# An 8192x8192 fp32 transpose: 16 KB store reads, and loads written as sixteen 512-byte runs into a column-major, 256-byte-aligned input buffer

## Chip, cores, metric

One core of one Trainium2 chip (trn2). The metric is device time in microseconds (us) of the whole kernel, as a median of several executions. Lower is better.

## The reference

```python
def setup_inputs():
    return {"x": np.random.randn(8192, 8192).astype(np.float32)}

def reference(x):
    return np.transpose(x)
```

256 MiB have to be read and 256 MiB written: 537 MB in all through the core's 16 DMA engines.

## The kernel before

The matrix is worked off in 32 blocks of 1024 rows x 2048 columns (8 MB). A block is loaded in two DMAs of 4 MB on the SP queue. The input buffer lies in SBUF, the core's memory of 128 partitions. In each partition a matrix row of 2048 floats is 8 KB, read in one piece and written in one piece. (A contiguous piece that a DMA writes is called a write run below.) The tensor engine (PE) transposes 128x128 squares against an identity into PSUM, the buffer that it writes; ScalarE (ACT) and VectorE (DVE) take turns to copy PSUM into `out_tile`; every four column groups ACT issues a 2 MB store. There are two input buffers and four output buffers.

```python
    R = 8;  C = 16;  I = R * P;  J = C * P;  G = 4;  LS = 2
    in_pool  = ctx.enter_context(tc.tile_pool(name="in_pool", bufs=2))
    out_pool = ctx.enter_context(tc.tile_pool(name="out_pool", bufs=4))
    # [...] const pool, PSUM pool of 4, identity
    for bj in range(n_bj):
        for bi in range(n_bi):
            in_tile = in_pool.tile([P, R, J], dt)                  # row-major
            rs = R // LS
            for s in range(LS):                                    # two loads of 4 MB
                src = x[i0 + s * rs * P:i0 + (s + 1) * rs * P, j0:j0 + J]
                src = src.rearrange("(a p) j -> p a j", p=P)
                nc.sync.dma_start(out=in_tile[:, s * rs:(s + 1) * rs, :], in_=src)
            for g in range(C // G):
                out_tile = out_pool.tile([P, G, I], dt)
                for bb in range(G):
                    # [...] 8 transposes of in_tile[:, a, b*P:(b+1)*P] into ps
                    # [...] ACT or DVE copies ps to out_tile[:, bb, :]
                dst = out[j0 + g * G * P:j0 + (g + 1) * G * P, i0:i0 + I]
                dst = dst.rearrange("(b q) i -> q b i", q=P)
                nc.scalar.dma_start(out=dst, in_=out_tile)         # 2 MB, 4 KB pieces
```

As built, a store's access patterns are `[[4096,128],[1024,4],[1,1024]]` on the SBUF side and `[[8192,128],[1048576,4],[1,1024]]` on the DRAM side: both sides in pieces of 1024 floats, 4 KB, although the SBUF side is one contiguous run of 16 KB in each partition. All SBUF tiles start 128 bytes past a multiple of 256.

## Time and profile before

| | before |
|---|---|
| time | 1278.35 us (1277.52 to 1279.18, 2 runs) |
| profiled span | 1276.3 us |
| bytes moved | 537.5 MB, mean 421 GB/s |
| DMA packets | 32768 of 8 KB (loads), 65536 of 4 KB (stores) |
| busy: PE / DVE / ACT | 55% / 25% / 20% |

The page of the kernel before. The DMA and GB/s lines have one entry for each fortieth of the span: the busy share of the 16 DMA engines in tenths, and what they moved. Under "DMA queue", q1 carries the loads and q10 the stores; the last column is the time that their packets took, as a share of 16 engines' span. Part 4 is the chain of work that ended last.

```profile
span 1276.3 us, 9511 instructions
...
DMA  9999999999999999999999999999999999999999
GB/s 392 425 423 424 425 423 425 423 422 424 423 422 423 424 424 423 424 422 423 424 424 422 422 422 424 424 423 423 423 423 424 422 422 422 424 424 423 422 422 375
...
q10 hardware_dynamic: 67584, 268.44, 51.4%
q1 hardware_dynamic: 33792, 268.44, 49.8%
...
DMA 89%; PE 6%; DVE 3%; issue 0%; ACT 0%; DVEq 0%; ACTq 0%; SPq 0%
...
```

The engines are busy in every slice, and the two queues' packets add up to 101.2% of the span, a little over 100% because neighbouring packets overlap. Apart from the first and last slice nothing is left but the rate itself, 422 to 425 GB/s.

Two stretches of the kernel before in the windows view (bounds in us, length, busy time and number of instructions of PE, of PE's weight loads, of DVE, ACT and POOL, then granted PE clock, DMA share, GB/s): a steady one and the last 37 us.

```profile
...
40.00:640.00 600.00, 332.62 (x1912) 298.34 (x1912) 145.36 (x120) 115.76 (x119) 0.00 (x0) 0.72 1.02 423
1240.00:1277.00 37.00, 15.20 (x126) 13.30 (x123) 9.80 (x8) 8.10 (x8) 0.00 (x0) 0.81 0.91 374
...
```

The longest waits of the kernel before (engine, line, what it waited for: us in total, times, longest):

```profile
...
ACT out_tile L69 <- DMA out_dram<-out_tile: 832.2, 97, 14.2
...
DVE out_tile L71 <- DMA out_dram<-out_tile: 593.7, 81, 11.7
...
PE ps L63 <- DMA in_tile<-in_x_dram: 25.0, 3, 13.0
...
```

The copies wait for stores to free an output buffer. PE almost never waits for input (25.0 us in 3 waits). So input is ahead of need and output is what lags.

Besides these views the trace records every DMA packet with its queue, start, size and duration. There is one data packet for each piece read, however it is written. They are remarkably uniform, and I use them throughout as "packet records": here 8 KB load packets have a median of 309 ns and 4 KB store packets one of 159 ns.

### The profile page before, as it was taken

How to read it: one execution, taken by the hardware profiler on the slowest of the kernel's cores; microseconds unless marked ns; L12 is line 12 of the kernel's file. 1: busy time of each engine (PE TensorE's matmuls, PEld its weight loads, DVE VectorE, ACT ScalarE, POOL GpSimd, SP SyncE). 2: the span in 40 equal slices, each digit the busy share in tenths (PEclk: the TensorE clock that was granted, in tenths of full speed). 3: DMA queues.
4: the chain of work that ended last, by engine and by line, in shares of the span. 5: the costliest groups of instructions: out<-in, count | busy, mean ns of one | idle time of the engine just before them, and what ended most of it. 6: DMA issues, size and time to landing. Idle time of an engine off the chain costs nothing.

```text
span 1276.3 us, 9511 instructions
## 1 busy us (share of the span) xinstructions
PE 700.7 (55%) x4096; PEld 629.0 (49%) x4096; DVE 313.5 (25%) x256; ACT 252.8 (20%) x257; POOL 0.7 (0%) x6
## 2 busy tenths in 40 slices
PE   3555555655565545655556555555555655556463
PEld 3454455544554544544445554454444544445453
DVE  1222223222232222322123221222222322122222
ACT  1221112121121211212112121221211212112121
POOL 0000000000000000000000000000000000000000
PEclk8777777767777677776677766878667777677867
DMA  9999999999999999999999999999999999999999
GB/s 392 425 423 424 425 423 425 423 422 424 423 422 423 424 424 423 424 422 423 424 424 422 422 422 424 424 423 423 423 423 424 422 422 422 424 424 423 422 422 375
DMA packets 101418, 537.49 MB, mean 421 GB/s; under 512 B 3072, under 2 KB 3072, under 8 KB 68608
## 3 DMA queue, kind: packets, MB, share of 16 engines
q10 hardware_dynamic: 67584, 268.44, 51.4%
q1 hardware_dynamic: 33792, 268.44, 49.8%
q8 instruction: 32, 0.52, 0.1%
q14 instruction: 10, 0.08, 0.0%
HBM read 268.44 MB, written 268.44 MB: 421 GB/s over the span
## 4 chain that ended last, share of the span: by engine, by line
DMA 89%; PE 6%; DVE 3%; issue 0%; ACT 0%; DVEq 0%; ACTq 0%; SPq 0%
DMA out_dram<-out_tile 87%; PE ps L63 6%; DVE out_tile L71 3%; DMA in_tile<-in_x_dram 2%; ACT out_tile L69 0%; DVEq L71 0%; ACTq L69 0%; SPq L55 0%
## 5 line engine op out<-in xcount | busy, mean ns | idle before, releaser
L63 PE MATMUL ps<-ident,in_tile 128*128 128x128 f32 x4096 | 700.7, 344 | 560.5 <-DVE out_tile L71 535.3
L63 PEld LDWEIGHTS ps<-ident,in_tile 128*128 128x128 f32 x4096 | 629.0, 181 | 631.9 <-DVE out_tile L71 605.9
L71 DVE COPY out_tile<-ps 128x1024 f32<-128x1024 f32 x256 | 313.5, 1225 | 948.9 <-DMA out_dram<-out_tile 593.7
L69 ACT COPY out_tile<-ps 128x1024 f32<-128x1024 f32 x256 | 251.5, 1014 | 1007.1 <-DMA out_dram<-out_tile 832.2
L69 ACT ACT_TABLE_LOAD x1 | 1.3, 1283 | 0.7 <-PEq L91 0.7
masks.py:199 POOL TENSOR_SCALAR_AFFINE_SELECT ident<-ident 128x128 f32<-128x128 f32 x1 | 0.3, 292 | 0.1
masks.py:197 POOL MEMSET ident<- 128x128 f32 x1 | 0.2, 204 | 0.3 <-POOLq L91 0.3
L91 POOL MEMSET const-bfloat16-1.0<- 128x1 bf16 x1 | 0.1, 101 | 0.0
L91 POOL MEMSET const-uint8-127<- 128x1 uint8 x1 | 0.1, 101 | 0.0
L91 POOL MEMSET const-float32-0.0<- 128x1 f32 x1 | 0.1, 98 | 0.2 <-issue 0.2
L91 POOL MEMSET const-float32-1.0<- 128x1 f32 x1 | 0.1, 98 | 0.0
## 6 DMA issues: line engine op xcount, KB each, us to landing
in_tile<-in_x_dram SPq DMA_DIRECT2D x64, 4096.0 KB, 27.9
out_dram<-out_tile ACTq DMA_DIRECT2D x128, 2048.0 KB, 28.9
```

Of the source, the lines that this page charges most:

```text
L63: nc.tensor.transpose(ps[:, a * P:(a + 1) * P], in_tile[:, a, b * P:(b + 1) * P], ident,)
L69: nc.scalar.copy(out=out_tile[:, bb, :], in_=ps)
L71: nc.vector.tensor_copy(out=out_tile[:, bb, :], in_=ps)
L91: nc = _bacc.Bacc("TRN2", target_bir_lowering=False, num_devices=1)
```

## The change

The intent: fewer, larger reads. A hand-made access pattern keeps the long contiguous side of a DMA as one run instead of cutting it to the pieces of the other side. Stores then read 16 KB at once and write four 4 KB rows. Loads still read 8 KB rows, but the input buffer is now column-major (`[P, C, R, P]`), so a row is written as sixteen 512-byte runs that are 4 KB apart. A pad of 128 bytes moves all tiles to multiples of 256 bytes. A block is loaded by eight DMAs of 1 MB instead of two of 4 MB. Waits are written by hand, with the same numbers of buffers. PE, ACT and DVE work is the same.

```diff
+def wide_dma(nc, eng, queue, out, in_):      # a DMA whose two sides keep their own run lengths
+    return eng.add_instruction(mybir.InstDMACopy(mode="Copy", [...],
+        ins=[physical(in_)], outs=[physical(out)], queue=queue))
-    LS = 2
+    LS = R
+        nc.alloc_sbuf_tensor("pad", [P, 32], dt)
-            in_tile = in_pool.tile([P, R, J], dt)
+        ins = [nc.alloc_sbuf_tensor(f"in_tile{k}", [P, C, R, P], dt).ap() for k in range(NIN)]
-                nc.sync.dma_start(out=in_tile[:, s * rs:(s + 1) * rs, :], in_=src)
+                src = x[i0 + s * P:i0 + (s + 1) * P, j0:j0 + J]
+                ld = wide_dma(nc, nc.sync, "qSPDynamicHW", in_tile[:, :, s, :], src)
-                            in_tile[:, a, b * P:(b + 1) * P],
+                            in_tile[:, b, a, :],
-                nc.scalar.dma_start(out=dst, in_=out_tile)
+                    st = wide_dma(nc, nc.scalar, "qActDynamicHW", dst, outs[ob])
 # [...] semaphores by hand instead of tile pools; the first block's loads and the last store
 # [...] use dma_start (the loads come out with the same access patterns)
```

More of the change, by code (lines that the diff above doesn't have):

```diff
@@ L8, with physical @@
 from concourse._compat import with_exitstack
+def physical(ap):
+    t = ap.tensor
+    dims = [list(d) for d in ap.ap]
+    if len(dims) == 2:
+        dims.insert(1, [dims[1][1], 1])
+    return mybir.PhysicalAccessPattern(
+        ap=dims,
+        offset=ap.offset,
+        dtype=ap.dtype,
+        memref=t.name,
+        memsetref=t.name + "_set",
+    )
+def wide_dma(nc, eng, queue, out, in_):
+    return eng.add_instruction(
+        mybir.InstDMACopy(
+            mode="Copy",
+            name=nc.get_next_instruction_name(),
+            engine=eng.engine,
+            ins=[physical(in_)],
+            outs=[physical(out)],
+            queue=queue,
+        )
+    )
 @with_exitstack
@@ L29 @@
     G = 4
-    LS = 2
-    const_pool = ctx.enter_context(tc.tile_pool(name="const", bufs=1))
-    in_pool = ctx.enter_context(tc.tile_pool(name="in_pool", bufs=2))
-    out_pool = ctx.enter_context(tc.tile_pool(name="out_pool", bufs=4))
-    psum_pool = ctx.enter_context(tc.tile_pool(name="psum", bufs=4, space=bass.MemoryType.PSUM))
-    ident = const_pool.tile([P, P], dt)
-    make_identity(nc, ident)
-    n_bi = N // I
-    n_bj = M // J
-    copy_idx = 0
-    for bj in range(n_bj):
-        j0 = bj * J
-        for bi in range(n_bi):
-            i0 = bi * I
-            in_tile = in_pool.tile([P, R, J], dt)
-            rs = R // LS
-            for s in range(LS):
-                src = x[i0 + s * rs * P:i0 + (s + 1) * rs * P, j0:j0 + J]
-                src = src.rearrange("(a p) j -> p a j", p=P)
-                nc.sync.dma_start(out=in_tile[:, s * rs:(s + 1) * rs, :], in_=src)
+    LS = R
@@ new lines @@
+    NIN = 2
+    NOUT = 4
+    NPS = 4
+    with tc.tile_critical():
+        nc.alloc_sbuf_tensor("pad", [P, 32], dt)
+        ident = nc.alloc_sbuf_tensor("ident", [P, P], dt).ap()
+        ins = [nc.alloc_sbuf_tensor(f"in_tile{k}", [P, C, R, P], dt).ap() for k in range(NIN)]
+        outs = [nc.alloc_sbuf_tensor(f"out_tile{k}", [P, G * I], dt).ap() for k in range(NOUT)]
+        pss = [nc.alloc_psum_tensor(f"ps{k}", [P, I], dt).ap() for k in range(NPS)]
+        s_id = nc.alloc_semaphore("s_id")
+        s_ld = [[nc.alloc_semaphore(f"s_ld{k}_{s}") for s in range(LS)] for k in range(NIN)]
+        s_st = [nc.alloc_semaphore(f"s_st{k}") for k in range(NOUT)]
+        s_pe = nc.alloc_semaphore("s_pe")
+        s_cp = [nc.alloc_semaphore("s_cpa"), nc.alloc_semaphore("s_cpv")]
+        nc.gpsimd.memset(ident, 0.0).then_inc(s_id, 1)
+        nc.gpsimd.wait_ge(s_id, 1)
+        nc.gpsimd.affine_select(
+            out=ident,
+            in_=ident,
+            compare_op=mybir.AluOpType.not_equal,
+            fill=1.0,
+            base=0,
+            pattern=[[-1, P]],
+            channel_multiplier=1,
+        ).then_inc(s_id, 1)
+        nc.tensor.wait_ge(s_id, 2)
+        blocks = [(bi, bj) for bj in range(M // J) for bi in range(N // I)]
+        rs = R // LS
+        n = 0
+        ng = 0
+        NG = len(blocks) * (C // G)
+        for k, (bi, bj) in enumerate(blocks):
+            slot, use = k % NIN, k // NIN
+            i0, j0 = bi * I, bj * J
+            in_tile = ins[slot]
+            if k >= NIN:
+                nc.sync.wait_ge(s_pe, (k - NIN + 1) * C)
+            for s in range(LS):
+                src = x[i0 + s * P:i0 + (s + 1) * P, j0:j0 + J]
+                if k > 0:
+                    ld = wide_dma(nc, nc.sync, "qSPDynamicHW", in_tile[:, :, s, :], src)
+                else:
+                    ld = nc.sync.dma_start(
+                        out=in_tile[:, :, s, :], in_=src.rearrange("p (b c) -> p b c", c=P)
+                    )
+                ld.then_inc(s_ld[slot][s], 16)
@@ L57 @@
             for g in range(C // G):
-                out_tile = out_pool.tile([P, G, I], dt)
+                ob, ouse = ng % NOUT, ng // NOUT
+                ng += 1
                 for bb in range(G):
                     b = g * G + bb
-                    ps = psum_pool.tile([P, R * P], dt)
+                    ps = pss[n % NPS]
+                    e = n % 2
+                    eng = (nc.scalar, nc.vector)[e]
+                    if n >= NPS:
+                        nc.tensor.wait_ge(s_cp[(n - NPS) % 2], (n - NPS) // 2 + 1)
@@ L62 @@
                     for a in range(R):
-                        nc.tensor.transpose(
+                        if b == 0 and a % rs == 0:
+                            nc.tensor.wait_ge(s_ld[slot][a // rs], 16 * (use + 1))
+                        ins_t = nc.tensor.transpose(
                             ps[:, a * P:(a + 1) * P],
-                            in_tile[:, a, b * P:(b + 1) * P],
+                            in_tile[:, b, a, :],
                             ident,
                         )
-                    if copy_idx % 2 == 0:
-                        nc.scalar.copy(out=out_tile[:, bb, :], in_=ps)
-                    else:
-                        nc.vector.tensor_copy(out=out_tile[:, bb, :], in_=ps)
@@ L72 @@
-                    copy_idx += 1
+                    ins_t.then_inc(s_pe, 1)
+                    eng.wait_ge(s_pe, n + 1)
+                    if bb < 2 and ouse > 0:
+                        eng.wait_ge(s_st[ob], 16 * ouse)
+                    o = outs[ob][:, bb * I:(bb + 1) * I]
+                    if e == 0:
+                        c = nc.scalar.copy(out=o, in_=ps)
+                    else:
+                        c = nc.vector.tensor_copy(out=o, in_=ps)
+                    c.then_inc(s_cp[e], 1)
@@ L74 @@
+                    n += 1
                 dst = out[j0 + g * G * P:j0 + (g + 1) * G * P, i0:i0 + I]
+                nc.scalar.wait_ge(s_cp[0], n // 2)
+                nc.scalar.wait_ge(s_cp[1], n // 2)
                 dst = dst.rearrange("(b q) i -> q b i", q=P)
-                nc.scalar.dma_start(out=dst, in_=out_tile)
+                if ng < NG:
+                    st = wide_dma(nc, nc.scalar, "qActDynamicHW", dst, outs[ob])
+                else:
+                    st = nc.scalar.dma_start(out=dst, in_=outs[ob])
@@ L80 @@
+                st.then_inc(s_st[ob], 16)
+        for ob in range(NOUT):
+            nc.sync.wait_ge(s_st[ob], 16 * (ng // NOUT))
 _INS = ['x']
```

## The prediction

> **What bounds it now.** The DMA engines. The page's slices show DMA at 9 (90% or more) in all 40, and 422 to 425 GB/s in all but the first (392) and last (375); 537.5 MB move in the 1276.3 us span. The chain of waits is 89% DMA, almost all stores. PE is busy 55%, DVE 25%, ACT 20%; their waits (ACT 832 us, DVE 594 us for stores to free out_tile) are consequences.
>
> The packet records behind the queue table are very regular: an 8 KB load packet takes 309 ns, a 4 KB store packet 159 ns, a 4-byte semaphore packet 9 ns. So 4 KB take 150 ns, and each packet of either direction has a fixed cost of about 9 ns. In the steady stretch busy time sums to 101.7%, so neighbours overlap by 3.6 ns and about 5.9 ns count. The Trainium skill, "DMA: Bandwidth & Descriptors", section "Where 436 GB/s comes from", puts the ceiling at 435.2 GB/s; the packets' slope agrees. Estimate: 537 MB at that rate 1233.6 us, plus 6144 data packets per engine x 5.9 ns = 36 us, plus 6 to 8 us of ramp and tail = 1276 to 1278. This closes.
>
> **What the change does.**
> 1. Stores read 16 KB at once instead of four times 4 KB: 1024 instead of 4096 read packets per engine. DRAM runs stay 4 KB. If the fixed cost belongs to the read packet: -3072 x 5.9 ns = -18 us, all on the critical path.
> 2. Loads keep 8 KB reads (2048 packets per engine) but write sixteen 512-byte runs each: 32768 write runs per engine instead of 2048. If a packet is cut on the read side and its writes stream, cost near 0. Each nanosecond per run that does not hide costs 33 us. I think most of it hides.
> 3. SBUF tiles start 256-aligned instead of 128 bytes off. The same page, section "How a descriptor splits into AXI transactions", says an unaligned start costs extra beats. The trace has no aligned data packets, only a few instruction packets of 8 KB at 307 instead of 309 ns. Estimate: 0 to 4 ns of the 5.9 for the 3072 remaining packets, 0 to -12 us, say -5.
> 4. 256 loads of 1 MB instead of 64 of 4 MB: 192 more semaphore packets per engine, at most +2 us. Issuing stays hidden on the SP queue.
> 5. PE, DVE and ACT work is unchanged (4096 transposes, 256 copies), buffering too (2 inputs, 4 outputs). If the queues alternate by packet, 16 KB store packets now beat 8 KB load packets, the reverse of before. Input arrives later, and waits move from "copies wait for stores" to "PE waits for loads"; the engines stay busy, so no time.
>
> **Sum.** 1278 - 18 - 5 + 2 + about 1 = **1258 us** (range 1244 to 1310). Faster by over 2% (below 1252.8): 0.31; within 2%: 0.46; slower by over 2%: 0.23.
>
> **What would show it.** Steady slices at 429 to 432 GB/s; store packets of 16 KB near 610 ns; load packets of 8 KB still at 305 to 309 ns (write runs free) or clearly longer, or recorded as 512-byte packets (not free); PE waits for in_tile grow, copies' waits for out_dram shrink.
>
> **What would make it wrong.** (a) Each 512-byte write run costs a beat or more: 1295 us at 1.2 ns, 1370 at 3.5 ns. (b) The fixed cost belongs to write runs for stores too: step 1 gives nothing. (c) Alignment was most of the 5.9 ns: about 1248. (d) Loads, held back by larger store packets, leave PE too little time (a block takes PE about 32 of its 40 us) and the engines run dry.

## The result

| | before | changed |
|---|---|---|
| time (median) | 1278.35 us | 1386.15 us (1382.26 to 1390.05, 2 runs) |
| ratio | 1 | 1.0838 (95% interval 1.0801 to 1.0875) |
| mean rate | 421 GB/s | 387 GB/s |
| load packets, median / mean | 309 / 309.8 ns | 342 / 353.3 ns |
| store packets, median / mean | 159 / 159.9 ns (4 KB) | 626 / 627.6 ns (16 KB) |

The changed kernel was executed twice, 8 us apart, and not again with the experiments, so a difference from it is uncertain by some 4 us.

It is 8.4% slower; the range ended at 1310 us. The page of the changed kernel, the lines that answer to those of before:

```profile
span 1388.3 us, 9561 instructions
...
DMA  9999999999999999999999999999999999999996
GB/s 339 404 396 392 382 388 401 406 389 376 378 397 399 394 385 389 394 394 400 388 386 392 401 395 391 381 399 401 392 395 392 380 392 391 371 380 398 397 405 258
...
q1 hardware_dynamic: 36864, 268.45, 52.3%
q10 hardware_dynamic: 18816, 268.44, 46.4%
...
SPq 95%; DMA 1%; PE 1%; issue 1%; DVE 0%
...
```

The engines are as busy as before and move less: 371 to 406 GB/s between the first slice and the last, and 258 in the last. The packets are fewer (q10 has 18816 instead of 67584, semaphore packets included), yet the loads' packets take 52.3% of a longer span, where they took 49.8%. The chain is no longer DMA: it is 95% "SPq", the SP queue issuing loads. That looks as if issuing were the limit; experiment 1 shows that it isn't.

The same two kinds of stretches, steady and last 49 us, of the changed kernel:

```profile
...
40.00:640.00 600.00, 243.94 (x1789) 228.03 (x1788) 136.63 (x113) 109.26 (x112) 0.00 (x0) 0.68 1.00 392
1340.00:1389.00 49.00, 17.30 (x123) 16.48 (x123) 9.79 (x8) 7.85 (x8) 0.00 (x0) 0.64 0.72 296
...
```

and its longest waits:

```profile
...
ACT out_tile L136 <- PE ps L125: 1113.3, 157, 29.5
...
PE ps L125 <- DMA in_tile<-in_x_dram: 813.1, 134, 7.5
ACT out_tile L136 <- DVE out_tile L138: 8.0, 3, 2.7
...
```

Waits have turned round. No copy waits for a store any more; PE waits 813.1 us for input, in 134 waits. Input is now what lags. In the last stretch the DMA share falls to 0.72, where before it was 0.91.

### The profile page after: what moved, and what is told of

Read it like the earlier page. It is cut to its first block, busy times and chain, and to the rows that moved or that the text cites. A ratio compares the mean times of both kernels' runs of the same rounds, so it can differ in the third digit from the quotient of the medians.

```text
span 1388.3 us, 9561 instructions
## 1 busy us (share of the span) xinstructions
PE 560.0 (40%) x4096; PEld 522.5 (38%) x4096; DVE 313.4 (23%) x256; ACT 251.3 (18%) x257; POOL 0.7 (0%) x6
## 3 DMA queue, kind: packets, MB, share of 16 engines
q1 hardware_dynamic: 36864, 268.45, 52.3%
q10 hardware_dynamic: 18816, 268.44, 46.4%
## 4 chain that ended last, share of the span: by engine, by line
SPq 95%; DMA 1%; PE 1%; issue 1%; DVE 0%
SPq L29 94%; SPq L108 1%; DMA in_tile<-in_x_dram 1%; PE ps L125 1%; DVE out_tile L138 0%; SPq L177 0%; SPq L64 0%
## 5 line engine op out<-in xcount | busy, mean ns | idle before, releaser
L125 PE MATMUL ps<-ident,in_tile 128*128 128x128 f32 x4096 | 560.0, 302 | 813.1 <-DMA in_tile<-in_x_dram 813.1
L125 PEld LDWEIGHTS ps<-ident,in_tile 128*128 128x128 f32 x4096 | 522.5, 156 | 850.3 <-DMA in_tile<-in_x_dram 843.6
```

The source lines that it names most:

```text
L125: ins_t = nc.tensor.transpose(ps[:, a * P:(a + 1) * P], in_tile[:, b, a, :], ident,)
```

## The experiments

The theories:

- **Theory 1, write runs.** A write run costs the DMA engines time even though the read is one 8 KB piece. The loads' packets are longer for that reason.
- **Theory 2, turns.** The two queues take turns by packet. With 16 KB store packets against 8 KB load packets the loads get a third of the bytes and not two thirds. Input is late, loads run alone for long stretches, and the last block is worked off with idle DMA engines.
- **Theory 3, issuing.** Suppose that each piece read or written has to be described to the DMA engines when SP issues a load. Then the 17 descriptors of a row (one read, sixteen writes) can't be made fast enough.

### 1. Loads alone, measured by themselves (`bench_loads`)

Its output is wrong, which doesn't matter for the time. Stretches of sixteen 1 MB loads, with waits in between, and nothing else on the queues:

```diff
+        phase(loads=(1, ...))    # runs per 8 KB row: 1, 1 (128 bytes off), 4, 8, 16,
+        phase(loads=(16, ...))   # 16 on two queues, 16 contiguous, 16 with 512-byte reads,
+                                 # 16 (128 bytes off), 32, 1 on two queues
```

> A measurement with wrong output on purpose: stretches of sixteen 1 MB loads and nothing else, all waited for between stretches. In order: 8 KB rows written as one run (aligned by hand-made access patterns), the same 128 bytes off, 4 runs of 2 KB, 8 of 1 KB, 16 of 512 bytes, 16 of 512 issued from two queues by turns, 16 of 512 that are contiguous in the buffer, 16 of 512 with reads of 512 too, 16 of 512 128 bytes off, 32 of 256, one run from two queues; stores of 4 KB come early as one stretch. Theory 1: packet time rises by 2 to 2.5 ns per run (309, 309, 316, 325, 344), the same from two queues and for contiguous runs. Theory 3 (the SP queue's descriptor generator can't make 17 descriptors per row fast enough): two queues bring 16 runs back to about 309 ns and 420 GB/s, and 512-byte reads, with 32 descriptors per row, take nearly twice as long as 17. Alignment: the stretches 128 bytes off are 0 to 4 ns per packet slower for one run.

The windows view of this kernel, one line for each stretch in that order (the stretch's bounds, its length, engines, then PE clock, DMA share, GB/s):

```profile
...
125.28:165.40 40.12, 0.00 (x0) 0.00 (x0) 1.00 1.00 418
167.20:208.10 40.90, 0.00 (x0) 0.00 (x0) 1.00 0.99 410
210.10:251.10 41.00, 0.00 (x0) 0.00 (x0) 1.00 1.00 409
252.90:295.50 42.60, 0.00 (x0) 0.00 (x0) 1.00 0.99 394
297.30:342.70 45.40, 0.00 (x0) 0.00 (x0) 1.00 0.99 370
344.50:389.40 44.90, 0.00 (x0) 0.00 (x0) 1.00 0.99 374
391.20:436.80 45.60, 0.00 (x0) 0.00 (x0) 1.00 0.99 368
438.70:488.10 49.40, 0.00 (x0) 0.00 (x0) 1.00 1.13 340
489.90:548.30 58.40, 0.00 (x0) 0.00 (x0) 1.00 1.00 287
550.20:606.90 56.70, 0.00 (x0) 0.00 (x0) 1.00 0.95 296
608.60:648.90 40.30, 0.00 (x0) 0.00 (x0) 1.00 1.00 416
...
```

| stretch | GB/s | median packet, ns |
|---|---|---|
| 1 run of 8 KB / 128 bytes off | 418 / 410 | 309 / 311 |
| 4 runs of 2 KB | 409 | 315 |
| 8 runs of 1 KB | 394 | 325 |
| 16 runs of 512 bytes / 128 bytes off | 370 / 287 | 344 / 455 |
| 16 runs, two queues by turns | 374 | 344 on both |
| 16 runs described, contiguous in the buffer | 368 | 344 |
| 16 runs, reads of 512 bytes too | 340 | 27 for 512 bytes |
| 32 runs of 256 bytes | 296 | 384 |

Theory 1 holds: from one run to sixteen a packet grows by 35 ns, 2.3 ns for each further run, and nearly evenly along the way. Nor do the runs have to be scattered: described as sixteen but adjacent, they cost the same. Theory 3 falls for these stretches. A second issuing queue gives 374 instead of 370 GB/s; that alone would leave a generator that both queues share. But 32 pieces for each row (reads of 512 bytes too) took only 9% longer than 17 (49.40 against 45.40 us), where theory 3 expected nearly twice the time, and the same 17 pieces took 29% longer when 128 bytes off (58.40 us). The issue instructions agree. The stretch's first load, into an empty queue, took SP 0.54 us to issue; from the fifth on most took 2.66 us, about the pace at which the engines finished loads (2.7 us apart), and 3.54 us when 128 bytes off. SP is solidly busy because it waits for room, not because it can't keep up.

Alignment, which I had put at 0 to 4 ns for a packet, costs 111 ns for a packet of sixteen short runs, and 2 ns in the median for one long run (that stretch was 2% longer, 40.90 against 40.12 us).

### 2. Row-major input, everything else as changed (`row_major`)

```diff
-        ins = [nc.alloc_sbuf_tensor(f"in_tile{k}", [P, C, R, P], dt).ap() ...]
+        ins = [nc.alloc_sbuf_tensor(f"in_tile{k}", [P, R, J], dt).ap() ...]
-                    ld = wide_dma(nc, nc.sync, "qSPDynamicHW", in_tile[:, :, s, :], src)
+                dst_in = in_tile[:, s, :]
+                    ld = wide_dma(nc, nc.sync, "qSPDynamicHW", dst_in, src)
 # [...] the first block's dma_start writes to dst_in too
-                            in_tile[:, b, a, :],
+                            in_tile[:, a, b * P:(b + 1) * P],
```

> The changed kernel, but each load row is written as one 8 KB run (row-major input buffer); stores, alignment, waits and load size as changed. Theory 1 (each 512-byte write run costs the DMA engines some 2 to 2.5 ns): load packets return to about 309 ns from 353, time 1250 to 1272 us, faster than or equal to before. Theory 2 (16 KB store packets take turns with 8 KB load packets, so input is late and the DMA engines idle): still at 1340 us or more, PE still waits over 600 us for in_tile.

Measured: 1285.45 us (1283.51 to 1287.98), ratio to before 1.0062 (1.0047 to 1.0077). Load packets are back at 309 ns (mean 311.0). So the input buffer's layout accounts for about 100 of the 108 us. But the expected time was missed, and it lies in neither theory's range: the version with wide stores, alignment and long write runs is still a little slower than before. Its steady and last stretches, and its waits:

```profile
...
40.00:640.00 600.00, 259.56 (x1921) 243.26 (x1921) 146.95 (x120) 117.13 (x120) 0.00 (x0) 0.70 1.01 427
640.00:1210.00 570.00, 241.96 (x1794) 226.62 (x1794) 137.16 (x112) 109.36 (x112) 0.00 (x0) 0.70 1.01 425
1210.00:1284.00 74.00, 32.53 (x249) 31.28 (x249) 19.59 (x16) 15.62 (x16) 0.00 (x0) 0.71 0.76 319
...
```

```profile
...
ACT out_tile L135 <- PE ps L124: 1015.9, 160, 28.1
...
PE ps L124 <- DMA in_tile<-in_x_dram: 714.2, 128, 7.3
...
```

It does move 425 to 427 GB/s where before moved 423. It loses that again at the end: 319 GB/s over the last 74 us costs 74 x (1 - 319/425) = 18 us against the steady rate; the last 37 us of before (374 against 423) cost 4 us. And PE waits 714 us for input, as in the changed kernel. That is theory 2, here with its price alone: about 14 us more at the end, of which the steady stretches pay back some 8 (an estimate: 1170 us x (1 - 423/426)). The profiled spans differ by 1283.1 - 1276.3 = 7 us.

### 3. Four runs, and eight (`runs_2k`, `runs_1k`)

```diff
-        ins = [... [P, C, R, P] ...]
+        ins = [... [P, C // W, R, W * P] ...]      # W = 4: runs of 2 KB; W = 2: 1 KB
-                            in_tile[:, b, a, :],
+                            in_tile[:, b // W, a, (b % W) * P:(b % W + 1) * P],
```

> The changed kernel with four 2 KB write runs per load row instead of sixteen of 512 bytes (input buffer in column groups of 512). Theory 1 with a cost per run: a quarter of the runs, so about a fifth of the gap between row_major and the changed kernel (3/15 of it): some 20 to 30 us above row_major, load packets about 315 to 320 ns. Theory 2: no difference from the changed kernel. If only runs below some length cost: as row_major.

> The changed kernel with eight 1 KB write runs per load row. A cost strictly per run, drawn from 1285 us at one run to 1386 at sixteen: 1332 us. From the load stretches measured alone (2.4 us more per 16 MB than one run, where sixteen runs took 5.3 us more): 1285 + 38 = 1323 us or less, less if four runs' small cost (5 us) means that the first runs hide. Load packets 325 ns.

| runs for each row | time, us | ratio to before | load packet in the mix, ns (mean) |
|---|---|---|---|
| 1 | 1285.45 | 1.0062 | 310.7 |
| 4 | 1290.51 | 1.0100 (1.0083 to 1.0117) | 313.5 |
| 8 | 1310.06 | 1.0250 (1.0234 to 1.0266) | 321.2 |
| 16 | 1386.15 | 1.0838 | 336.8 |

("In the mix" are the microseconds in which packets of both queues run. The edit has a side effect: the first of the 32 blocks, loaded with dma_start, is now also read in pieces of 2 or 1 KB, which costs about 2 and 3 us by the packet records.) For four and eight runs the steps are 5 and 25 us over one run, below what an even cost over the whole range would give (20 and 47 us). The last step, from eight to sixteen, is 76 us, three quarters of the total. I had expected too much for the first runs. The packets' medians alone grow evenly in experiment 1, so the jump at the end suggests that something besides the run cost comes in between eight and sixteen. (It is in the records: see the 24 us under step 2 below.)

### 4. Stores of before beside the changed loads (`narrow_stores`)

```diff
-                    st = wide_dma(nc, nc.scalar, "qActDynamicHW", dst, outs[ob])
+                st = nc.scalar.dma_start(out=dst, in_=outs[ob].rearrange("q (b i) -> q b i", b=G))
 # [...] the other branch, for the last store, goes
```

> The changed kernel with the stores of before (four 4 KB reads), only the loads changed. If wide stores save 3072 fixed costs of 5.9 ns per engine beside such loads: about 1386 + 18 = 1404 us. If turns between the queues matter (theory 2), smaller store packets bring the input in earlier and the time falls by 10 us or more, to 1376 or less.

Measured: 1343.64 us (1343.14 to 1344.86), ratio 1.0518 (1.0502 to 1.0533). Taking the wide stores away makes the changed kernel 43 us faster, as theory 2 had it (1376 us or less); the prediction's step 1 says 18 us slower. The waits, in this kernel:

```profile
...
ACT out_tile L136 <- DMA out_dram<-out_tile: 1016.2, 121, 13.2
...
PE ps L125 <- ACT out_tile L136: 621.3, 109, 11.1
...
```

They are turned back: copies wait for stores again, and PE for copies. The packet records say what that does to the engines' work. I sorted every microsecond by whether store packets took under 5% of the engines' time in it (loads alone), load packets did, or neither:

| kernel | loads alone: us, GB/s, mean load packet | both: us, GB/s, mean load packet |
|---|---|---|
| before | 30 us, 412, 317 ns | 948 us, 423, 309 ns |
| changed | 385 us, 347, 370 ns | 951 us, 408, 337 ns |
| row_major | 308 us, 425, 311 ns | 928 us, 425, 311 ns |
| narrow_stores | 34 us, 371, 351 ns | 1040 us, 399, 334 ns |

The rest is almost all stores alone: some 295 us in before and 261 in narrow_stores, at 416 to 418 GB/s, but only 35 to 40 in the other two. (All these figures shift by up to a few per cent with how a packet that crosses a microsecond is counted.)

While both queues have work, they get about as many packets each, as if they took turns: 31200 load packets to 35494 store packets in such microseconds of before, 16531 to 15389 in the changed kernel. (The records don't name the engine, so the order on one engine isn't seen.) Before, a turn was 8 KB of load against 4 KB of store; now it is 8 against 16. So before, loads were ahead (SP waited 1099.6 us for PE to free an input buffer) and stores were left to run alone; now stores finish early, and 385 us remain in which loads have the engines to themselves. For one-run loads that is harmless (425 GB/s). For sixteen-run loads it is the worst case: 347 GB/s.

### 5. Even turns (`col_store8k`)

```diff
-                    st = wide_dma(nc, nc.scalar, "qActDynamicHW", dst, outs[ob])
+                    st = wide_dma(nc, nc.scalar, "qActDynamicHW", dst,
+                                  outs[ob].rearrange("q (h i) -> q h i", h=2))   # 8 KB store reads
```

> The changed kernel (sixteen 512-byte write runs) with store reads of 8 KB instead of 16 KB, so that loads and stores take even turns and there are few stretches of loads alone. If the run cost in the mix is all that is left (measured alone: 58 to 67 us over one run per row): 1277 + 58 to 67 = 1335 to 1347 us. If 16 KB store reads were innocent and only run count matters: 1380 us or more. Stretches of loads alone fall from 385 us to under 100 us.

Measured: 1355.6 us (1354.05 to 1357.9), ratio 1.0608 (1.0593 to 1.0622). Loads alone fell to 81 us as expected. The time is 9 us over the range I gave, but 30 us under the changed kernel, only because a store's read is 8 KB and not 16. Turns are thus part of the cause, and the rest (1355.6 against 1277.4 for the same with one run, experiment 7) is the cost of the runs.

### 6. Loads and stores measured by themselves (`bench_mixed`)

Its output is wrong, which doesn't matter for the time. Stretches of sixteen loads (16.8 MB), sixteen 2 MB stores (33.6 MB), or both:

```diff
+        phase(stores=...)               # 4 KB reads; the same 128 bytes off; 16 KB reads
+        phase(loads=..., stores=...)    # 1 run and 4 KB; 128 bytes off; 1 run and 16 KB;
+                                        # 4 runs and 16 KB; 16 and 16 KB; 16 and 4 KB
+        # [...] and 16 KB stores 128 bytes off, alone and with loads; 16 contiguous and 16 KB
```

> A measurement with wrong output on purpose: stretches of sixteen 1 MB loads, sixteen 2 MB stores, or both at once, waited for in between. In order: loads of one run; stores of four 4 KB reads, the same 128 bytes off; stores of one 16 KB read, the same 128 bytes off; then loads of one run together with 4 KB stores, the same 128 bytes off, with 16 KB stores, the same 128 bytes off; loads of 4 runs with 16 KB stores; of 16 runs with 16 KB stores; of 16 runs with 4 KB stores; of 16 contiguous runs with 16 KB stores. My prediction's step 1 (5.9 ns saved for each read packet saved) says 16 KB stores alone run at about 430 GB/s against 420 for 4 KB ones, and the same gap in the mix. If the fixed cost of a packet is hidden by its neighbour, the gap in the mix is under 1%. Write runs: beside 16 KB stores a load of 16 runs and the store beside it take 35 to 45 ns more together than with one run, so the mix falls to about 410 GB/s.

The windows view, one line for each of the nine stretches in the order of the first three comment lines:

```profile
...
43.66:123.54 79.88, 0.00 (x0) 0.00 (x0) 1.00 1.02 420
124.90:208.45 83.55, 0.00 (x0) 0.00 (x0) 1.00 1.01 402
210.32:289.05 78.73, 0.00 (x0) 0.00 (x0) 1.00 1.00 426
371.71:492.28 120.57, 0.00 (x0) 0.00 (x0) 1.00 1.02 417
493.66:614.50 120.84, 0.00 (x0) 0.00 (x0) 1.00 1.01 417
616.32:736.28 119.96, 0.00 (x0) 0.00 (x0) 1.00 1.00 420
859.76:979.61 119.85, 0.00 (x0) 0.00 (x0) 1.00 1.00 420
981.45:1105.61 124.16, 0.00 (x0) 0.00 (x0) 1.00 1.00 405
1107.11:1231.35 124.24, 0.00 (x0) 0.00 (x0) 1.00 1.02 405
...
```

The three stretches not shown: 16 KB stores 128 bytes off took 79.46 us alone and 119.82 with loads of one run, and sixteen contiguous runs with 16 KB stores 124.21. Wide stores alone ran at 426 where step 1 says about 430, the gap in the mix was under 1% as expected if the fixed cost is hidden, and sixteen runs in the mix ran at 405 where I expected about 410. Each figure is of one stretch.

Three readings:

- **Wide store reads.** Alone, 16 KB reads take 78.73 us where 4 KB reads take 79.88. That is 1.15 us for 33.6 MB; the kernel stores eight times as much, so 9 us and not 18. Beside loads it is 0.61 us (120.57 to 119.96), or 5 us for the kernel. The DMA share shows where the other half went: 4 KB packets are busy 1.02, 16 KB ones 1.00. Much of a small packet's fixed cost lies under its neighbour, and that overlap goes when the packets go.
- **Write runs in the mix.** Sixteen runs cost 4.2 us (119.96 to 124.16) for 16.8 MB of loads, or 67 us for the kernel's sixteenfold; beside 4 KB stores 3.7 us, or 59 us. That answers to narrow_stores, which is 63 us slower than the same with row-major loads (1343.64 against 1280.23, experiment 7). Four runs cost nothing in the mix (119.85).
- **Alignment.** The stretch of 4 KB stores 128 bytes off ran at 402 GB/s, the aligned one at 420. But that is not shown to be alignment's: where the same stores ran alone at the end of their mixed stretch (558 to 613 us, after its loads), the packet records give 421 GB/s and 159 ns a packet, as when aligned. Beside loads nothing is lost (417 and 417; with 16 KB stores 420 and 420). The kernel before, with its tiles 128 bytes off, has 159 ns in its 295 us of stores alone too. So the pad would bring the kernel before next to nothing; row_narrow_stores in experiment 7 is much like it but aligned, and is not faster.

### 7. Wide stores with the turns mended (`row_narrow_stores`, `row_store8k`, `row_tail_narrow`, `best_8k_tail`)

All four have row-major loads. The stores are: 4 KB reads throughout; 8 KB reads; 16 KB reads but 4 KB in the last two of the 32 blocks; 8 KB reads but 4 KB in the last four.

```diff
 # row_tail_narrow; best_8k_tail has 4 * and the 8 KB reads of row_store8k
-                if ng < NG:
+                if ng < NG - 2 * (C // G):
                     st = wide_dma(nc, nc.scalar, "qActDynamicHW", dst, outs[ob])
                 else:
-                    st = nc.scalar.dma_start(out=dst, in_=outs[ob])
+                    st = nc.scalar.dma_start(out=dst, in_=outs[ob].rearrange("q (b i) -> q b i", b=G))
```

> Row-major loads of one 8 KB run and the stores of before (four 4 KB reads), aligned, 1 MB loads. Theory 2 (16 KB store packets win the turns, so input comes late and the last block is worked off with idle DMA engines): the poor last two slices of row_major go, which were worth about 13 us; wide stores gave 0.5% in the steady slices (425 to 428 against 423), about 6 us, which go too unless alignment gave them. So 1270 to 1280 us. Prediction's step 1: 1285 + 18 = 1303 us.

> row_major with store reads of 8 KB instead of 16 KB, the same size as a load packet. Theory 2: turns are even, loads are late by less; the tail is between: 1272 to 1283 us, PE waits for in_tile well below the 714 us of row_major. Prediction's step 1 (fixed cost per read packet): 1285 + 6 = 1291.

> row_major with 16 KB stores for all blocks but the last two, which store with 4 KB reads, so that the last loads win the turns again. Theory 2: the steady slices stay at 425 to 428 GB/s, the last slices recover half or more of the 13 us: 1270 to 1279 us. If the tail has another cause: 1285.

> row_store8k (one 8 KB write run per load row, store reads of 8 KB) with the stores of the last four of 32 blocks read in 4 KB pieces, so that loads win the turns before the end. row_store8k ran at 427 GB/s in its steady slices against 423 of before, and lost about 15 us in its last two slices (385 and 267). If late input is all that the tail is: last slices as before, time 1266 to 1272 us, ratio 0.991 to 0.995. If the tail stays for another reason: 1277 us.

| kernel | store reads | time, us | ratio to before |
|---|---|---|---|
| row_narrow_stores | 4 KB | 1280.23 | 1.0015 (0.9998 to 1.0031) |
| row_major | 16 KB | 1285.45 | 1.0062 (1.0047 to 1.0077) |
| row_tail_narrow | 16 KB, last blocks 4 KB | 1277.39 | 1.0000 (0.9977 to 1.0024) |
| row_store8k | 8 KB | 1277.38 | 0.9994 (0.9979 to 1.0009) |
| best_8k_tail | 8 KB, last blocks 4 KB | 1274.05 | 0.9968 (0.9956 to 0.9981) |

row_tail_narrow and row_store8k came within the times expected, row_narrow_stores ended 0.2 us above its range, and best_8k_tail missed its range by 2 us. best_8k_tail beats both kernels, before by 0.3%, which is within 2% and so counts as the same. Its two stretches:

```profile
...
40.00:640.00 600.00, 266.39 (x1920) 244.50 (x1920) 146.60 (x120) 117.12 (x120) 0.00 (x0) 0.69 1.01 427
1240.00:1273.00 33.00, 8.14 (x71) 7.43 (x69) 7.06 (x6) 5.78 (x6) 0.00 (x0) 0.74 0.73 298
...
```

Even turns give the full 427 GB/s in the steady part. The last 33 us still run at 298: they cost 33 x (1 - 298/427) = 10 us, more than the 4 us of before, so part of the tail stays and I did not find out why. row_store8k did not bring PE's wait for input down as I had expected: it is 676.5 us, against 714.2 in row_major. So the time fell by 8 us while the wait hardly changed: how long PE waits does not by itself set the time. What did change is the time of loads alone, 308 us in row_major and about 51 here.

### 8. The pad taken away (`col_unaligned`)

```diff
-        nc.alloc_sbuf_tensor("pad", [P, 32], dt)
```

> The changed kernel without the 128-byte pad, so that every SBUF tile starts 128 bytes off a multiple of 256, as in the kernel before. In the stretches alone an unaligned load of sixteen runs took 455 ns per packet against 344 aligned, one of one run 311 against 309. If that carries over: about 110 ns x 2048 = 227 us more, 1560 to 1620 us. If alignment matters as little as the prediction had it: 1386 to 1400 us.

Measured: 1477.15 us (1476.01 to 1478.4), ratio 1.1558 (1.1542 to 1.1573). The pad saves the changed kernel 91 us. My figure of 227 us assumed that all loads pay. The packet records show that only loads alone do: their mean there is 456 ns instead of 370. In the mix it is 342 instead of 337. (16200 packets x 86 ns / 16 engines are 87 of the 91 us.)

## Why the prediction was wrong

**What bounds the kernel: right.** It is DMA-bound before and after. The sum of packet times described both kernels (for each engine 1293.2 us in a span of 1276.3 before, 1372.1 in 1388.3 after).

**Step 2, "I think most of it hides": wrong, and the step that failed.** The prediction gave the sixteen write runs a cost near zero and kept 1295 to 1370 us as a case against it. Alone, a run costs 2.3 ns, and little of that hides: in the mix a load packet grows by 26 ns and the store packet beside it by 10, together 2.4 ns for each further run. On the prediction's own scale (33 us for each nanosecond) 2.3 ns are 76 us, so that its 1258 us become 1334; most of the 52 us left belong to steps 1 and 5 below. Between row_major and the changed kernel, which differ in nothing but this, the profiled span grows by 1388.3 - 1283.1 = 105 us. From the packet records, divided by the 16 engines:

| term | us |
|---|---|
| loads in the mix: 16531 packets, mean 310.7 to 336.8 ns | 27 |
| stores of 16 KB: 16256 packets, mean 617.3 to 627.6 ns | 10 |
| loads alone, the regular part: 16220 packets, median 309 to 344 ns | 35 |
| loads alone, further growth of the mean (2.4 to 26.1 ns over the median) | 24 |
| not in packets: idle engines or lost overlap | about 8 |

The first three terms, 72 us, are the run cost as measured by itself: the stretches of experiments 1 and 6 give 84 us if all loads ran alone (45.40 - 40.12 = 5.28 us, times sixteen) and 67 if all ran in the mix, so about 76 for half and half. The 24 us are packets much longer than usual: of the loads-alone packets 9.6% took over 400 ns, where row_major has under 1% and the kernel with eight runs 0.6%. They come in bunches. In the first 40 us there are seven clusters of 10 to 15 such packets within a microsecond. In each of the thirty later stretches of loads alone the rate dips 2 to 4 us after the stores have ended: on average from 372 GB/s to 295 and 263 in the third and fourth microsecond. About 40% of the long packets' extra time falls there, and most of the rest at the stretch's end; the engines' share dips too, to 0.88 and 0.90, which makes some 7 of the 8 us not in packets. row_major (427) and eight runs (407) have no such dip. The cause is open. That SP's lead is short with such loads fits (it runs two to three loads ahead, and up to ten with one run for each row), since SP's issues are 7.5 us apart in the mix and 2.7 us alone. But in the stretch of experiment 1 SP's lead is as short, and only 3.1% of packets took over 400 ns; no run here separates the lead from other causes.

**Step 1, "-3072 x 5.9 ns = -18 us, all on the critical path": right in kind, too large.** The engines' packet time did fall by 18 us: in row_major it sums to 1274.9 us for each engine, against 1293.2 before. But the span did not follow. In the steady stretch the packets' times added up to 101.7% of it before and to 100.9% in row_major, so that about 10 us of the 18 had been overlap with a neighbour; and after 1200 us the engines are idle for 17 us in row_major against 2 before, which is step 5. Measured by itself, step 1 is worth 9 us alone and 5 us in the mix. The 5.9 ns was an average over the kernel's mix. It is not what one packet less saves.

**Step 5, "the engines stay busy, so no time": its first half right, its conclusion wrong.** The turns did reverse, and waits moved from stores to input just as described (PE's wait for in_tile from 25 to 813 us; ACT's wait for stores from 832 us to none). But late input is not free. It leaves too little to overlap in the last block (about 14 us in row_major) and it moves half the loads out of the mix into stretches of their own, where their write runs cost most. With both together, 16 KB store reads cost the changed kernel 43 us against 4 KB ones (1386.15 against 1343.64), where with row-major loads they cost 5 (1285.45 against 1280.23). The 38 us between belong to neither change alone; 24 of them are the long packets whose cause is open. In that sense most of the price of the turns is measured (experiments 4 and 5) and not explained.

**Step 3, alignment: mis-sized for short runs.** In the kernel before it is worth nothing measurable, in the changed kernel 91 us. The prediction scaled it by packets; alone it cost 2 ns for a packet of one run and 111 ns, or 7 ns for each run, for a packet of sixteen.

**Step 4, more semaphore packets: right.** They took 2.3 us instead of 0.6 on each engine.

The sign to watch did its work: "load packets of 8 KB still at 305 to 309 ns (write runs free) or clearly longer". They were longer, and row_major put them back at 309.

## What to carry to other kernels

Look at the shorter side of a DMA: here 8 KB reads written in 512-byte runs loaded at 370 GB/s, against 340 with 512 bytes on both sides and 418 with 8 KB on both, and at 287 when the runs started 128 bytes off. Where two queues were both full here they got about as many packets each, so a packet's size was also that queue's weight; make the larger packets those whose lateness hurts, and check the last block and the stretches where one queue runs alone. A fixed cost got from dividing a total by a count is not the saving for one packet less: measure both sizes alone and in the mix. And a test of one suspect (here a second issuing queue) can leave a rival standing: look for a stretch in which the suspect's work changes and the rival's does not.

## What the Trainium skill lacked or had wrong

- "DMA: Bandwidth & Descriptors", section "Why small descriptors are slow (HBM only)", puts the fixed cost at about 3 cycles for each packet and says that joining descriptors into packets is only worth it up to 256 bytes. It gives no time for a write run: inside one 8 KB read packet each further run cost 2.3 ns (309 ns with one, 344 with sixteen). Reading 8 KB at once instead of sixteen times 512 bytes, with the same runs written, raised loads from 340 to 370 GB/s; that is a longer descriptor and not a joining of short ones, so the page's limit is not tested here.
- The same page's table "Specifications" gives 512 bytes as the least transfer for line rate. Write runs of 512 bytes ran at 370 GB/s, of 1 KB at 394, of 2 KB at 409, of 8 KB at 418.
- The same page, section "How a descriptor splits into AXI transactions", explains unaligned starts and counts beats for two sizes, but gives no times. Starting 128 bytes off cost 2 ns in the median for a run of 8 KB, 111 ns for sixteen of 512 bytes, and nothing measurable for long runs in a mix of loads and stores.
- The same page, section "Queues, rings and completion order", says that queues take turns by packet; the trace's counts agree (16531 load and 15389 store packets in the mixed time), though the page's packet holds several descriptors and the trace's is one read piece. It lacks the consequence: the queue with the longer reads wins the bytes (8 KB against 16 KB gave 385 us of loads alone).
- "Perfetto Trace Analysis", section "What "DMA-bound" means", takes an issuing track that is solid with DMA slices for descriptor generation. Here SP's issues were 95% of the chain, yet 32 pieces for each row instead of 17 took only 9% longer, a second queue changed 370 to 374 GB/s, and an issue into an empty queue took 0.54 us where those into a full one took 2.66.
